# Output projection of a hybrid decoder: first readings copied by ACT, x added by DMA, low weight parts by DMA, norm scaled on demand

## The chip, the cores and the metric

The kernel runs on one core of a Trainium2 chip. The metric is the time of one execution on the device in microseconds (us); three runs of the kernel before gave 2228.88, 2226.73 and 2226.81 us, median 2226.81.

The engines by their names in the profile: PE is the matrix engine (PEld its weight loads), DVE the vector engine, ACT the scalar engine, POOL GpSimd, SP the engine that issues most DMAs. All DMAs are carried out by 16 DMA engines. DMAs that SP issues are plain copies; those that POOL issues here add their source to what stands at the destination (accumulate), on a queue of their own.

## The reference

```
for l in range(DEPTH):                      # DEPTH = 2, SEQ = D_MODEL = 1024
    h = rmsnorm(x, norm_mix_g[l])
    ... = split_cols(h @ w_in[l])           # gMLP, Mamba-2 SSD and MLA branches
    mix = concatenate([y_a, y_b, y_c])      # 1024 wide
    x = x + mix @ w_out[l]                  # the output projection
    x = x + squared_relu_mlp(rmsnorm(x, norm_mlp_g[l]), mlp_w1[l], mlp_w2[l])
return rmsnorm(x, final_norm_g)

def squared_relu_mlp(h, w1, w2):            # w1: 1024 x 4096, w2: 4096 x 1024
    return square(relu(h @ w1)) @ w2
```

All in float32.

## The kernel before

Everything is kept with features on the partitions: x is eight tiles of 128 features x 1024 tokens. Each layer has a front (norm, input projection, gMLP, SSD, attention) and then nine large products of 1024 x 1024 by 1024 x 1024, which L998 runs: the output projection `w_out` (stage 0) and, for each of four quarters of the hidden width, `w1` and `w2` (stages 1 to 8).

**A stage** (class `Stage`) is one such product by a scheme of seven block products in place of eight. Weight and activation are cut into quadrants; the seven products, numbered 1 to 7, use quadrants or running sums of quadrants, and `done(p, os)` reads the four PSUM accumulators `os` after product p and adds or subtracts them where they belong. `LATE1` and `EARLY1` are the two orders of the products; stage 0 has LATE1 (1, 5, 6, 3, 7, 2, 4), stage 1 EARLY1 (1, 2, 5, 6, 3, 7, 4). Each product has two halves kh = 0, 1. One half is a step: 4 accumulators x 2 x 3 = 24 matmuls of 128x128 by 128x512. A step is named (stage, number), number 0 to 13; (0, 10) is the first half of product 2 of the output projection. Products 1, 2, 4 and 7 load their weights into `raw` tiles (product 7 by a load and an accumulating DMA), product 5 into a tile `ssum`, which accumulating DMAs then turn into the weights of 6 and 3.

**High and low parts.** For accuracy each float32 operand is split into a high part in the type float32r, rounded (`act.copy`), and a low part, the difference (`tt(lo, src, f(hi), subtract)` on DVE). That is `split` (L114). The matmuls are high weight by high activation, high weight by low activation, low weight by high activation, in this order; so the low part of the weight (`wlo`) is read by the third matmul of a step.

**Run** (class `Run`) goes through the steps of all nine stages. Before step i it prepares weights (`prep_w`) and activations (`prep_b`) up to step i + AHEAD = i + 2. `hooks` are calls after given steps: `norm_r(0)` after (0, 10), `norm_x(0)` after (0, 11), `norm_r(1)` after (1, 0), `norm_x(1)` after (1, 1).

**x and the norm.** `mlp` loads the eight x tiles through SP (L1071) at the start of the projection. `add_to` adds each reading of stage 0 to x on DVE: 4 readings after products 1, 5, 6, 3, 2 and 4 and 8 after product 7, 32 per layer. x is complete by halves of the tokens: half 0 after product 7, half 1 after product 4. Then `after_mix` squares it (ACT) and sums the squares (DVE, POOL); `norm_r` sums over the partitions with eight small matmuls (`pss`) and takes the reciprocal root with thirteen small DVE operations (`rstd`, tiles `rv`, `ry`, `rt`); `norm_x` spreads it with eight matmuls (`rb`), copies that to SBUF (ACT), and scales all eight tiles of the half into `hB` on DVE. Stage 1 reads `hB`, half 0 from its first product, half 1 from product 5 on.

**What is scarce.** Common tiles of 128 x 1024 (`G`, 32 of them) hold x, the mixer's output, all high and low parts and sums of squares; `raw` has 4 tiles; PSUM has 8 banks, 4 with the tag "a", which the accumulators of some products, `pss` and `rb` share.

**What sets the order.** The program is written once in order of the calls; a scheduler then fixes each engine's instruction order before the run, by its own estimate of times and by free tiles and banks. On the chip each engine and each DMA queue works strictly in that fixed order.

Of the kernel before, what the change touches and what calls it, by code (L numbers as in the profile page):

```python
# [18 lines left out]
P = 128  # L19
# [42 lines left out]
SETS = ("aaaa", "bbcc")  # L62
AHEAD = 2
MIX_FROM = 36


@with_exitstack
def trunk(ctx, tc, x, w_zdk, w_uv, w_f, w_q, w_kv, w_out, w1, w2, gains, pcol, prow, w_s, cst, out):
# [182 lines left out]
    def sq_rstd(acc, tag, t0=0, t1=NT, tg="c"):  # L251
        n = t1 - t0
        pss = bank(tg, "pss")
        for t in range(t0, t1):
            for i, q in enumerate(acc):
                mm(pss[:, t * 2:t * 2 + 2], q[:, t * P:(t + 1) * P], ones[:, 0:2], i == 0, i == len(acc) - 1)
        acc.clear()
        return rstd(pss[:, 2 * t0:2 * t1:2], n, tag)
# [642 lines left out]
    class Stage:  # L901


        def __init__(self, w, src, order, done, flip=False, chain=True, tmp=None):
            self.w, self.src, self.order, self.done, self.flip = w, src, order, done, flip
            self.fresh = (1, 2, 5) if chain else (1, 2, 4, 5)
            self.tmp = tmp or (lambda name: G(F32, name))
            self.s, self.t, self.held = [None] * 2, [None] * 2, {}

# [3 lines left out]
        def prep_w(self, p, kh):  # L913
# [6 lines left out]
            hi, lo = G(F32R, "whi"), G(F32R, "wlo")  # L920
            split(hi, lo, v)
            if p in (5, 6):
# [44 lines left out]
    class Run:  # L967
        def __init__(self, stages, hooks, end):
            self.steps, self.ready, self.hooks, self.end = [], [], hooks, end
            par = 0  # L970
# [6 lines left out]

        def prep(self, n):
            while len(self.ready) < min(n, len(self.steps)):
                st, p, kh = self.steps[len(self.ready)][:3]  # L980
                self.ready.append((st.prep_w(p, kh), st.prep_b(p, kh)))

        def go(self):
            for i, (st, p, kh, v, at) in enumerate(self.steps):
                self.prep(i + 1 + AHEAD)
                (wh, wl), (bh, bl) = self.ready[i]
# [22 lines left out]
    def add_to(xt, flip=False, chain=True, hook=None):  # L1009
# [4 lines left out]
        def done(p, os):  # L1014
# [4 lines left out]
            if hook:  # L1019
                hook(p)  # L1020

        return done
# [42 lines left out]
    def mlp(L, l, xsrc):  # L1065
# [3 lines left out]
        xt = [G(F32, "x") for _ in range(KD)]  # L1069
        for m in range(KD):  # L1070
            nc.sync.dma_start(out=xt[m], in_=xsrc[m * P:(m + 1) * P, :])  # L1071
        hB, scr = [], [BIG(F32, "scr")]
        acc, rs = {}, {}
# [9 lines left out]
        def norm_r(n):  # L1083
            rs[n] = sq_rstd(acc[n], "m", n * 4, n * 4 + 4, "a")

        def norm_x(n):
            if not hB:
                scr.clear()
                hB.append(BIG(F32, "hB").rearrange("p (k t) -> p k t", k=KD))
            o = bank("a", "rb")  # L1090
            half_bcast(rs.pop(n), o)
            rb = G(F32, "rb")
            act.copy(rb[:, 0:512], o)
            for m in range(KD):
                stt(hB[0][:, m, half(n)], xt[m][:, half(n)], gcol[:, 2 * l + 1, m:m + 1], rb[:, 0:512], ALU.mult, ALU.mult)

# [82 lines left out]

        class LazyB:  # L1180
            def __getitem__(self, k):
                return hB[0][k]

        stages = [Stage(w_out[l], mix_half, LATE1, add_to(xt, True, False, after_mix), True, False, scratch)]
        for q in range(NQ):
            end = q == NQ - 1
            stages.append(Stage(w1[l, q], halves_of(LazyB()), EARLY1 if q == 0 else LATE1, relu_to(Lazy())))
            stages.append(Stage(w2[l, q], halves_of(Lazy()), LATE1,
# [3 lines left out]
        if last:  # L1192
            hooks[8, 10] = [lambda: close_r(1)]
            hooks[8, 11] = [lambda: close_x(1, 0)]

        def end():
# [157 lines left out]
```

## Time and profile before

| | before |
|---|---|
| median of three runs | 2226.81 us |
| the profiled execution | 2227.68 us |
| its span | 2225.8 us |
| busy PE / DVE / ACT / POOL | 2180.0 / 1669.2 / 1131.5 / 470.9 us |
| DMA | 222.15 MB, 39.5% of 16 engines |
| output projection and stage 1, layer 0 | about 394 to 573 us |
| the same, layer 1 | about 1490 to 1668 us |

The span is the profiler's own time from first to last instruction; the rest of the profiled execution lies around it. Busy shares are averages over stages with different limits; where PE stands is read from its waits and from the chain that ended last. The times in the trace count from the start of the span. The granted clock is a share of 2.4 GHz.

### The profile page before, as it was taken

The numbers are of one execution on the slowest core, as the hardware profiler recorded it, in microseconds if no ns is written. First come the engines' busy times: TensorE is split into PE (matmuls) and PEld (weight loads), VectorE is DVE, ScalarE is ACT, GpSimd is POOL, SyncE is SP. The second block draws the span as 40 slices with busy tenths as digits, with TensorE's granted clock in tenths as the row PEclk, the third lists the DMA queues.
The fourth block names the chain that finished last, engine by engine and source line by source line (L and its number), as shares of the span: only waits on it lengthen the run. The fifth ranks groups of instructions, "written<-read, shape, count | busy, mean of one in ns | idle before, by whom it ended". The sixth has DMA issues, their size and how long they took to land.

```text
span 2225.8 us, 28714 instructions
## 1 busy us (share of the span) xinstructions
PE 2180.0 (98%) x10844; PEld 1854.6 (83%) x10844; DVE 1669.2 (75%) x2516; ACT 1131.5 (51%) x1841; POOL 470.9 (21%) x444
## 2 busy tenths in 40 slices
PE   9999999999999999999999999999899999999996
PEld 8888989877888888888898888988788888888885
DVE  6788688788775876767847868878888767677576
ACT  6363577545445445355534626774464453543543
POOL 3152266121010001001301613751110010001011
PEclk9999999999999999999999999999999999999998
DMA  5211301354555546535412112023565465456532
GB/s 182 65 53 57 86 1 71 82 132 102 126 132 136 122 104 144 147 90 121 154 49 69 60 45 67 1 98 74 123 153 122 104 142 142 105 109 147 131 67 76
DMA packets 63625, 222.15 MB, mean 100 GB/s; under 512 B 7456, under 2 KB 7552, under 8 KB 63488
## 3 DMA queue, kind: packets, MB, share of 16 engines
q0 software_dynamic: 20736, 75.51, 19.6%
q1 hardware_dynamic: 42752, 144.83, 19.6%
q8 instruction: 85, 1.39, 0.2%
q14 instruction: 52, 0.43, 0.1%
HBM read 211.87 MB, written 8.44 MB: 99 GB/s over the span
## 4 chain that ended last, share of the span: by engine, by line
PE 94%; DVE 2%; issue 2%; ACT 1%; DMA 0%; POOL 0%; POOLq 0%; SPq 0%; ACTq 0%; DVEq 0%
PE st L998 61%; PE cqkv L119 5%; PE xbc L119 5%; PE uvps L119 4%; PE av L119 4%; PE sc L119 3%; PE zps L119 2%; PE pTp L789 2%; PE qps L119 2%; PE yps L119 1%; PE vps L119 1%; PE knps L119 1%; PE rb L119 1%; DVE mx L751 1%; DMA x<-in_x 0%
## 5 line engine op out<-in xcount | busy, mean ns | idle before, releaser
L998 PE MATMUL st<-blo,whi 128*128 128x512 f32 x2016 | 787.2, 390 | 0.0
L998 PE MATMUL st<-bhi,wlo 128*128 128x512 f32 x2016 | 786.6, 390 | 0.0
L998 PE MATMUL st<-bhi,whi 128*128 128x512 f32 x2016 | 781.4, 391 | 2.4 <-ACT bhi L115 2.4
L998 PEld LDWEIGHTS st<-bhi,whi 128*128 128x128 f32 x2016 | 380.5, 189 | 81.3 <-ACT bhi L115 2.7
L998 PEld LDWEIGHTS st<-bhi,wlo 128*128 128x128 f32 x2016 | 380.2, 189 | 79.1
L998 PEld LDWEIGHTS st<-blo,whi 128*128 128x128 f32 x2016 | 380.5, 189 | 78.3
L192 POOL DMA_DIRECT2D ssum<-in_w x96 | 84.2, 883 | 923.8 <-DVE wlo L100 380.5
L100 DVE TENSOR_TENSOR wlo<-raw,whi 128x1024 fp32r<-128x1024 f32 (+3 forms) x188 | 239.0, 1272 | 53.9 <-issue 29.8
L100 DVE TENSOR_TENSOR x<-x,st 128x512 f32<-128x512 f32 x296 | 196.0, 680 | 32.9 <-PE st L998 32.5
L115 ACT CAST bhi<-tsum 128x1024 fp32r<-128x1024 f32 x96 | 101.0, 1052 | 215.0 <-DVE tsum L100 173.9
L115 ACT CAST whi<-raw 128x1024 fp32r<-128x1024 f32 (+3 forms) x188 | 193.8, 1034 | 16.2 <-DVE blo L100 12.7
L107 POOL TENSOR_SCALAR p<-p,sm 128x1024 f32<-128x1024 f32 (+6 forms) x84 | 158.9, 1901 | 113.7 <-DVE sm L774 81.8
L115 ACT CAST whi<-ssum 128x1024 fp32r<-128x1024 f32 x108 | 113.5, 1051 | 112.2 <-PE st L998 57.1
L100 DVE TENSOR_TENSOR wlo<-ssum,whi 128x1024 fp32r<-128x1024 f32 x108 | 131.8, 1220 | 49.7 <-ACT whi L115 27.6
L100 DVE TENSOR_TENSOR blo<-tsum,bhi 128x1024 fp32r<-128x1024 f32 x96 | 117.3, 1222 | 46.4 <-ACT bhi L115 46.0
L119 PE MATMUL av<-pT,vhi 128*128 128x256 f32 x480 | 113.5, 298 | 0.8 <-DVE pT L100 0.5
L1043 ACT ACTIVATE hid<-hid 128x1024 f32<-128x1024 f32 x64 | 67.9, 1061 | 84.3 <-DVE hid L1036 84.0
L1036 DVE CUSTOM_DVE_ANT_0 hid<-st,hid 128x512 f32<-128x512 f32 x96 | 65.2, 686 | 56.8 <-PE st L998 56.5
L119 PE MATMUL sc<-B 96*128 96x384 f32 (+11 forms) x432 | 101.0, 351 | 3.1 <-ACT p L764 1.8
L100 POOL TENSOR_TENSOR sq<-sq 128x512 f32<-128x512 f32 (+1 forms) x37 | 60.7, 1647 | 191.9 <-ACT sq L1055 179.9
L100 DVE TENSOR_TENSOR blo<-hB,bhi 128x1024 fp32r<-128x1024 f32 x48 | 58.7, 1223 | 48.5 <-ACT bhi L115 48.5
L764 ACT ACTIVATE p<-sc,mx 128x512 f32<-128x512 f32 (+3 forms) x144 | 83.2, 583 | 21.0 <-DVE mx L100 14.2
(244 smaller groups left out, 3647.2 us busy)
## 6 DMA issues: line engine op xcount, KB each, us to landing
raw<-in_w SPq DMA_DIRECT2D x128, 512.0 KB, 3.7
ssum<-in_w POOLq DMA_DIRECT2D x96, 512.0 KB, 5.7
ssum<-in_w SPq DMA_DIRECT2D x32, 512.0 KB, 4.5
raw<-in_w POOLq DMA_DIRECT2D x32, 512.0 KB, 9.3
raw<-in_w_f SPq DMA_DIRECT2D x20, 512.0 KB, 3.5
x<-in_x SPq DMA_DIRECT2D x16, 512.0 KB, 6.9
raw<-in_w_out SPq DMA_DIRECT2D x16, 512.0 KB, 3.7
dec<-adr SPq DMA_DIRECT2D x16, 384.0 KB, 3.5
```

What stands on the lines that cost most here:

```text
L100: (eng or dve).tensor_tensor(out=o, in0=a, in1=b, op=op)
L107: (eng or dve).tensor_scalar(out=o, in0=a, scalar1=s1, scalar2=None, op0=op0)
L115: act.copy(hi, src)
L119: pe.matmul(o, lhsT=l, rhs=r, start=start, stop=stop)
L192: pool.dma_start(out=o, in_=src, accum_op=ALU.add)
L751: dve.reduce_max(mx[:, n:n + 1], on, axis=AX.X, negate=True)
L764: act.activation(pw[:, n * wh:(n + 1) * wh], os[n][:, :wh], AF.Exp, bias=mx[:, 0:1], accum_out=sm[:, n:n + 1])
L789: pe.transpose(pt[:, c0:c0 + P], pp[j][:, kt * P:(kt + 1) * P], ident)
L998: pe.matmul(os[j], lhsT=w[:, cw], rhs=b[:, cb], start=first and n == 0, stop=last and n == 2, skip_group_check=True)
L1036: dve._custom_dve(TENSOR_ADD_SAT, out=d, in0=os[j], in1=d, s0=0.0 if full[0] else BIGGEST, s1=-BIGGEST if full[0] else 0.0)
L1043: act.activation(d, d, AF.Square)
```

## The change

Six edits, all in the output projection (stage 0) and the first MLP product (stage 1) of each layer.

1. `make` takes the place of `add_to` in stage 0. The first reading of each quadrant (after products 1, 5, 6 and 7) is copied from PSUM into the x tile by ACT, with the sign; then an accumulating DMA on POOL's queue adds the old x from memory. The second readings (after 3, 7, 2 and 4) are added by DVE as before. The eight loads of x through SP are gone.
2. In stages 0 and 1 (`by_dma`) the low parts of the weights of products 1, 2, 4 and 7 are no longer a DVE subtraction: ACT writes the negated high part into `wlo` and an accumulating DMA adds the weight, from memory, or for product 7 from the raw tile.
3. `norm_x` no longer scales the eight tiles at once; `normed` scales two tiles when a step of stage 1 first asks for them.
4. `norm_r` and `norm_x` use one PSUM bank for `pss` and `rb` where they had one each.
5. `Run.prep` prepares weights and activations with separate leads; before the steps in `SHORT` the activations are prepared one step ahead instead of two.
6. One tile `rb` is kept for both halves.

```diff
--- before.py
+++ after.py
@@ -61,6 +61,7 @@
 SAME = {LATE1: (0, 1, 0, 1, 0, 1, 0), EARLY1: (0, 1, 1, 0, 1, 0, 0)}
 SETS = ("aaaa", "bbcc")
 AHEAD = 2
+SHORT = ((0, 9), (0, 10), (0, 11), (0, 13), (1, 0), (1, 1))
 MIX_FROM = 36
 
 
@@ -250,7 +251,7 @@
 
     def sq_rstd(acc, tag, t0=0, t1=NT, tg="c"):
         n = t1 - t0
-        pss = bank(tg, "pss")
+        pss = bank(tg, "pss") if isinstance(tg, str) else tg
         for t in range(t0, t1):
             for i, q in enumerate(acc):
                 mm(pss[:, t * 2:t * 2 + 2], q[:, t * P:(t + 1) * P], ones[:, 0:2], i == 0, i == len(acc) - 1)
@@ -905,6 +906,8 @@
             self.w, self.src, self.order, self.done, self.flip = w, src, order, done, flip
             self.fresh = (1, 2, 5) if chain else (1, 2, 4, 5)
             self.tmp = tmp or (lambda name: G(F32, name))
+            self.parts = None
+            self.by_dma = False
             self.s, self.t, self.held = [None] * 2, [None] * 2, {}
 
         def b(self, b, n, kh):
@@ -918,7 +921,12 @@
             else:
                 v = self.s[kh]
             hi, lo = G(F32R, "whi"), G(F32R, "wlo")
-            split(hi, lo, v)
+            if self.by_dma and p in (1, 2, 4, 7):
+                act.copy(hi, v)
+                act.activation(lo, f(hi), AF.Copy, scale=-1.0)
+                gather(lo, v if p == 7 else self.w[LOADS[p][0] + (kh,)])
+            else:
+                split(hi, lo, v)
             if p in (5, 6):
                 gather(v, self.w[0, p - 5, kh])
             elif p == 3:
@@ -966,7 +974,7 @@
 
     class Run:
         def __init__(self, stages, hooks, end):
-            self.steps, self.ready, self.hooks, self.end = [], [], hooks, end
+            self.steps, self.w, self.ready, self.hooks, self.end = [], [], [], hooks, end
             par = 0
             for n, st in enumerate(stages):
                 sets = [par ^ v for v in SAME[st.order]]
@@ -975,14 +983,18 @@
                     for kh in range(2):
                         self.steps.append((st, p, kh, v, (n, 2 * i + kh)))
 
-        def prep(self, n):
-            while len(self.ready) < min(n, len(self.steps)):
+        def prep(self, n, m=None):
+            while len(self.w) < min(n, len(self.steps)):
+                st, p, kh = self.steps[len(self.w)][:3]
+                self.w.append(st.prep_w(p, kh))
+            while len(self.ready) < min(m or n, len(self.steps)):
                 st, p, kh = self.steps[len(self.ready)][:3]
-                self.ready.append((st.prep_w(p, kh), st.prep_b(p, kh)))
+                self.ready.append((self.w[len(self.ready)], st.prep_b(p, kh)))
+                self.w[len(self.ready) - 1] = None
 
         def go(self):
             for i, (st, p, kh, v, at) in enumerate(self.steps):
-                self.prep(i + 1 + AHEAD)
+                self.prep(i + 1 + AHEAD, i + 1 + (1 if at in SHORT else AHEAD))
                 (wh, wl), (bh, bl) = self.ready[i]
                 self.ready[i] = None
                 fresh = p in st.fresh
@@ -1021,6 +1033,27 @@
 
         return done
 
+    def make(xt, xsrc, flip, hook):
+        first = {1: (0, 0), 5: (1, 1), 6: (0, 1), 7: (1, 0)}
+        then = {3: (0, 1), 7: (1, 1), 2: (0, 0), 4: (1, 0)}
+
+        def done(p, os):
+            if p in then:
+                a, n = then[p]
+                for j in range(4):
+                    v = xt[a * 4 + j][:, half(n ^ flip)]
+                    tt(v, v, os[j], ALU.subtract if a else ALU.add)
+            if p in first:
+                a, n = first[p]
+                for j in range(4):
+                    m = a * 4 + j
+                    v = xt[m][:, half(n ^ flip)]
+                    act.activation(v, os[j], AF.Copy, scale=-1.0 if a else 1.0)
+                    gather(v, xsrc[m * P:(m + 1) * P, half(n ^ flip)])
+            hook(p)
+
+        return done
+
     def relu_to(hid):
         def done(p, os):
             def v(a, n, j):
@@ -1067,9 +1100,7 @@
         mix = L.mixA + L.mixC
         L.mixA = L.mixC = None
         xt = [G(F32, "x") for _ in range(KD)]
-        for m in range(KD):
-            nc.sync.dma_start(out=xt[m], in_=xsrc[m * P:(m + 1) * P, :])
-        hB, scr = [], [BIG(F32, "scr")]
+        hB, rb, have, scr = [], [], set(), [BIG(F32, "scr")]
         acc, rs = {}, {}
         slot = [0]
 
@@ -1081,18 +1112,28 @@
             return [mix[b * 4 + kh * 2 + kk][:, half(n)] for kk in range(2)]
 
         def norm_r(n):
-            rs[n] = sq_rstd(acc[n], "m", n * 4, n * 4 + 4, "a")
+            o = bank("a", "rb")
+            rs[n] = sq_rstd(acc[n], "m", n * 4, n * 4 + 4, o), o
 
         def norm_x(n):
             if not hB:
                 scr.clear()
                 hB.append(BIG(F32, "hB").rearrange("p (k t) -> p k t", k=KD))
-            o = bank("a", "rb")
-            half_bcast(rs.pop(n), o)
-            rb = G(F32, "rb")
-            act.copy(rb[:, 0:512], o)
-            for m in range(KD):
-                stt(hB[0][:, m, half(n)], xt[m][:, half(n)], gcol[:, 2 * l + 1, m:m + 1], rb[:, 0:512], ALU.mult, ALU.mult)
+                rb.append(G(F32, "rb"))
+            r, o = rs.pop(n)
+            half_bcast(r, o)
+            act.copy(rb[0][:, half(n)], o)
+
+        def normed(b, n, kh):
+            m0 = b * 4 + kh * 2
+            for m in range(m0, m0 + 2):
+                if (m, n) not in have:
+                    have.add((m, n))
+                    stt(hB[0][:, m, half(n)], xt[m][:, half(n)], gcol[:, 2 * l + 1, m:m + 1], rb[0][:, half(n)],
+                        ALU.mult, ALU.mult)
+            if len(have) == 2 * KD:
+                rb.clear()
+            return (hB[0][:, m0:m0 + 2, half(n)],)
 
         def after_mix(p):
             if p == 3:
@@ -1177,14 +1218,10 @@
                     hid.append(BIG(F32, "hid").rearrange("p (k t) -> p k t", k=KD))
                 return hid[0][k]
 
-        class LazyB:
-            def __getitem__(self, k):
-                return hB[0][k]
-
-        stages = [Stage(w_out[l], mix_half, LATE1, add_to(xt, True, False, after_mix), True, False, scratch)]
+        stages = [Stage(w_out[l], mix_half, LATE1, make(xt, xsrc, True, after_mix), True, False, scratch)]
         for q in range(NQ):
             end = q == NQ - 1
-            stages.append(Stage(w1[l, q], halves_of(LazyB()), EARLY1 if q == 0 else LATE1, relu_to(Lazy())))
+            stages.append(Stage(w1[l, q], normed, EARLY1 if q == 0 else LATE1, relu_to(Lazy())))
             stages.append(Stage(w2[l, q], halves_of(Lazy()), LATE1,
                                 add_to(xt, False, not end, (finish if last else to_next) if end else None), chain=not end))
         hooks = {(0, 10): [lambda: norm_r(0)], (0, 11): [lambda: norm_x(0)],
@@ -1192,6 +1229,9 @@
         if last:
             hooks[8, 10] = [lambda: close_r(1)]
             hooks[8, 11] = [lambda: close_x(1, 0)]
+
+        for st in stages[:2]:
+            st.by_dma = True
 
         def end():
             if not last:
```

## Rows read from the trace of the kernel before

**Rows 1.** The page: the chain that ended last, by engine.

```profile
PE 94%; DVE 2%; issue 2%; ACT 1%; DMA 0%; POOL 0%; POOLq 0%; SPq 0%; ACTq 0%; DVEq 0%
```

**Rows 2.** PE's waits, layer 0 and 1 (waiter, releaser: total us, times, longest).

```profile
PE rb L119 <- DVE ry L103: 7.0, 2, 4.6
...
PE rb L119 <- DVE ry L103: 7.0, 2, 4.5
```

**Rows 3.** DVE in order of time (start us, us, instruction, idle before it).

```profile
447.17 0.69 DVE L100 TENSOR_TENSOR x<-x,st 128x512 f32<-128x512 f32 x1 [0.67 <-PE st L998]
448.53 0.69 DVE L100 TENSOR_TENSOR x<-x,st 128x512 f32<-128x512 f32 x1 [0.67 <-PE st L998]
...
455.89 2.47 DVE L100 TENSOR_TENSOR x<-x,st 128x512 f32<-128x512 f32 x4
...
469.86 0.69 DVE L100 TENSOR_TENSOR x<-x,st 128x512 f32<-128x512 f32 x1 [0.66 <-PE st L998]
...
471.45 1.18 DVE L100 TENSOR_TENSOR rt<-ry 128x4 f32<-128x4 f32 x1
...
478.55 5.39 DVE L103 SCALAR_TENSOR_TENSOR hB<-x,gcol,rb 128x512 f32<-128x512 f32 x8 [2.85 <-ACT rb L1093]
```

**Rows 4.** The chain in order of time (start us, us, what).

```profile
475.76 2.08 PE rb L119 x8
477.84 23.71 PE st L998 x96
...
504.77 1.27 PE rb L119 x8
506.04 599.93 PE st L998 x2640
...
1135.32 0.89 PE rb L119 x8
```

**Rows 5.** Stretch, us, busy PE, PEld, DVE, ACT, POOL, granted clock, DMA share, GB/s.

```profile
452.00:506.00 54.00, 47.02 (x210) 39.10 (x209) 44.23 (x74) 23.69 (x32) 7.27 (x7) 0.93 0.54 137
```

**Rows 6.** Groups of instructions (busy us, mean ns of one, idle before).

```profile
L100 DVE TENSOR_TENSOR x<-x,st 128x512 f32<-128x512 f32 x296 | 196.0, 680 | 32.9 <-PE st L998 32.5
...
L100 DVE TENSOR_TENSOR wlo<-ssum,whi 128x1024 fp32r<-128x1024 f32 x108 | 131.8, 1220 | 49.7 <-ACT whi L115 27.6
...
L1039 ACT COPY hid<-st 128x512 f32<-128x512 f32 x96 | 56.0, 583 | 31.5 <-PE st L998 31.0
```

**Rows 7.** SP's queue and POOL in order of time.

```profile
376.69 7.43 SPq L1071 DMA_DIRECT2D x<-in_x  x8
...
390.14 5.97 POOL L107 TENSOR_SCALAR p<-p,sm 128x896 f32<-128x896 f32 x2 [1.58 <-DVE sm L774]
...
475.23 1.78 POOL L192 DMA_DIRECT2D ssum<-in_w  x2
```

**Rows 8.** DMA view, 390 to 452, 547 to 571: packets, MB, share; landing.

```profile
ssum<-in_w_out POOLq DMA_DIRECT2D x4, 512.0 KB, 5.8
...
q0 software_dynamic: 720, 2.62, 56.4%
q1 hardware_dynamic: 766, 2.74, 31.5%
...
ssum<-in_w POOLq DMA_DIRECT2D x3, 512.0 KB, 9.4
```

**Rows 9.** ACT and PE in order of time.

```profile
391.07 1.06 ACT L115 CAST whi<-raw 128x1024 fp32r<-128x1024 f32 x1
...
394.29 0.50 PE L998 MATMUL st<-bhi,whi 128*128 128x512 f32 x1 [1.19 <-ACT bhi L115]
...
449.79 1.03 ACT L115 CAST whi<-raw 128x1024 fp32r<-128x1024 f32 x1
```

**Rows 10.** DMA view, 452 to 506: packets, MB, share of 16 engines.

```profile
q1 hardware_dynamic: 1440, 5.24, 30.6%
q0 software_dynamic: 576, 2.10, 22.7%
```

## Prediction, made before the changed kernel was built or run

> **What bounds the kernel now.** I read the chain of work first: PE makes up 94% of the chain [rows 1]. In such a kernel time is won only where PE stands or runs slowly, so the next view is PE's waits, stretch by stretch. The change touches the output projection and the first MLP stage of each layer, and there PE waits for one thing: the broadcast of the norm (tile `rb`) waits for the reciprocal root `ry` on DVE, twice in each layer, 7.0 us together, the longer one 4.6 us [rows 2]. The reader is to see there that both layers show the same pair.
>
> The cost of these waits is more than their idle time. One accumulator j takes 6 matmuls, and at full clock DVE gets the next one every 1.36 us (447.17 and 448.53) [rows 3], so a matmul takes 0.2267 us and a step (24 matmuls, one half of one of the seven products) 5.44 us. Behind the first wait the eight broadcast matmuls take 2.08 us, where a pair without a wait takes 0.89, and the next 96 matmuls take 23.71 us instead of 96 x 0.2267 = 21.76 [rows 4]. The granted clock shows why: a mean of 0.93 from 452 to 506 us [rows 5], so part of that stretch ran at 1.2 and not 2.4 GHz. First wait: 4.6 + 1.19 + 1.95 = 7.7 us. Second: 2.4 + (1.27 - 0.89) + (599.93 - 2640 x 0.2267) = 2.4 + 0.4 + 1.4 = 4.2 us [rows 2, 4]. That is 11.9 us in layer 0; layer 1 has the same two waits [rows 2] and I give it the same, 23.8 us in all, 1.07% of the time. Nothing else in the stages concerned can give time back, since PE is otherwise fed.
>
> **The change part by part.** *The norm.* The last product of each half of x is added by DVE, then come squares, the sums `pss` on PE, thirteen small DVE operations, and `rb`. In the first wait x additions stood between the small operations (469.86), some of which took 1.18 us (471.45), and `rb` could start only at 475.76 [rows 3, 4]; in the second the same chain took the bare 2.4 us of the wait [rows 2]. After the change product 7 has four DVE additions instead of eight, 4 x 0.60 us less (the four at 455.89 took 2.47 us together [rows 3]), and the two low parts that DVE made just there are gone too (1.22 us each [rows 6]). The squares are so ready about 2.4 us sooner, which brings `pss` from the middle of step (0,11) towards its start, with nearly a whole step (5.44 us) for a chain of 2.4 to 4 us. The bank that `pss` and `rb` now share is one allocation less between product 7 and product 4, so the matmuls of the next step can be placed ahead of a late `rb`. For the second norm the eight scalings in one piece of 5.39 us (478.55) [rows 3] become two before each step that needs them; these are the same operations, spread out, and DVE has room: 44.23 us busy of 54 [rows 5], and it loses more than it gains. I cost the scaling at zero and expect both waits to go: minus 11.9 us per layer. With a lead of one step in place of two for six operand preparations (SHORT), copy, subtraction and two scalings (1.05 + 1.22 + 2 x 0.7 = 3.7 us) must fit in 5.44 us; queued behind them on DVE are only the additions of that step. Zero, and up to 1 us per layer if they queue badly.
>
> *x by DMA.* 16 DVE additions (680 ns) per layer become 16 ACT copies (583 ns [rows 6]) and 16 accumulating DMAs of 256 KB on POOL's queue; eight loads of 512 KB leave SP's queue at 376.69 [rows 7]. ACT is busy 23.69 us of 54 [rows 5] and gets 4 copies and 8 further passes there, 4 x 0.58 + 8 x 1.05 = 10.7 us: covered. Each x piece is added to again only two steps later at the earliest (product 6, then 3), 10.9 us for an accumulating DMA that alone lands 5.8 us after its issue [rows 8]: covered.
>
> *Low parts by DMA.* Per layer 16 DVE subtractions become 16 ACT passes (about 1.05 us [rows 9]) and 16 accumulating DMAs of 512 KB. The matmul that reads the low part is the third of its step, so the wait that is added stands in PE's own queue. The tightest place by time alone is step (0,10): high part at 449.79 [rows 9], need at 448.5 + 2 x 5.44 + 0.45 = 459.8. Copy, negation and landing take 1.05 + 1.05 + 5.8 = 7.9 us: on time by 2 us, if the DMA finds the engines free. POOL gets 32 further issues of about 0.9 us per layer (its two at 475.23 took 1.78 [rows 7]), in order behind its square sums.
>
> The engines are not free, and this is my main term. An accumulating DMA of 512 KB (a gather, as the code calls it) occupies the 16 DMA engines for longer than a load: from 452 to 506 four gathers made 22.7% of 54 us, 3.06 us each, and ten loads 30.6%, 1.65 each [rows 10]. Where the engines are crowded (547 to 571, share 56.4 + 31.5%), five gathers took 2.71 us each, and 766 packets (144 to a load) 1.42 us per load, and landing stretched from 5.8 to 9.4 us [rows 8]; the work of both queues adds up there. I use the crowded values. From 452 to step (1,3) the new kernel has 4 old gathers, the low parts of eight steps, (0,10) to (1,3), and four x pieces of half size: 14 x 2.71 = 37.9 us, with at least 8 of the ten loads, 11.4 us: 49.3 us. Of the lone landing of 5.8 us some 2.7 are no transfer; I put 1.4 ahead of it and 1 behind. So it starts at about 451.9 + 1.4 = 453.3 and has landed near 503.6. Without waits step (1,3) would need its low part at 506.04 - 10.5 + 5.44 + 0.5 = 501.5 (10.5 is 11.9 less the 1.4 lost behind 506): late by 2.1 us at least. By order it can be worse: ahead of the low part of step (1,0) stand four low parts, the x pieces, and the two gathers that POOL issued at 475.23 [rows 7]: 9 x 2.71 + 7 loads x 1.42 = 34.3 us, landed at 488.6, needed at 477.84 + 1.95 + 2 x 5.44 - 7.7 + 0.45 = 483.4, 5.2 us late; four gathers on, step (1,2) adds 1.3. If those two gathers go behind it, it is on time. So PE stands still 2.1 to 6.5 us per layer; middle 4.3. Such a stand costs clock too: 1.8 us behind the wait of 2.4 us, 3.1 behind the one of 4.6 (above), none if it comes in small pieces. I take 1.8. Given back: 6.1 us of 11.9 per layer, so 5.8 us net, 11.6 for both. The bounds: 2.1 + 0 leaves 19.6 us net, 6.5 + 3.1 leaves 4.6.
>
> *The sum.* The profiled execution took 2227.68 us around a span of 2225.8, 0.9 above the median; the differences are taken off the median: 2226.8 - 11.6 = **2215**, between 2207 and 2222.
>
> **The rivals.** *All of it is won.* Both waits go and each low part lands after the lone 5.8 us [rows 8], since PE needs it only 9.9 us or more after its high part starts. 2226.8 - 23.8 = 2203, 2200.6 with the 1.19 us as well that PE stands at the first step of each layer [rows 9]. Against it: the landing of 9.4 us where queues were full. The Trainium skill (DMA: Bandwidth & Descriptors, Anatomy of one DMA) fits a gpsimd DMA by 2.0 us + bytes / 436e3, an estimate of 3.2 us for 512 KB. By that this rival would hold and the time would be 2203; the trace shows 5.8 us, and 2.7 us of engine time in a crowd, so I follow the rows.
>
> *Nothing moves.* The order on PE is fixed before the run. If `pss` and `rb` keep their places, the waits stay and hide the late low parts, since 52 us of DMA work fits in the old 54. 2222 to 2231.
>
> *Slower: the first step's low part.* Step (0,0) begins at 394.29 [rows 9]. Its high part was cast at 391.07; negated by 393.1, its DMA would stand behind POOL's scaling until 396.1 [rows 7] and land at 401.9, needed at 394.8: 7.1 us, with 3.1 of clock 10.2 us per layer. With 6.1 given back later, that is 16.3 - 11.9 = 4.4 us per layer lost: 2236. It decides if the cast stays at 391. Against it: eight tiles of the common pool no longer go to x at 376.69 [rows 7], so cast and negation can be done some 10 us sooner.
>
> **How the numbers follow.** Part won 0.38 (2207 to 2222), all won 0.27 (2200 to 2207), nothing moves 0.12 (2222 to 2231), slower 0.23 (2231 to 2241). A measurement of this kernel tells 0.2%, 4.5 us, from no change. Faster is 0.38 + 0.27 = 0.65, the same 0.12, slower 0.23. From 2200 to 2235 leaves out some 0.14 above and 0.03 below. The likeliest alone is 2215.
>
> **What would show it.** Right: PE's waits no longer name `rb <- ry`, but `st` waiting for the DMA of `wlo` near steps (0,12), (1,0) and (1,2); the DMA share from 452 on is above 0.85; gathers land in 7 to 12 us. All won: no PE wait over 1 us, clock 1.00 throughout. Wrong: `rb` still waits, or the first wait of `st` is at the start of the projection. If the DMA share stays near 0.6, my engine times for a gather are too long.

## The result: slower by 1.3%, and the profile after

The changed kernel took 2257.98 us (median of four runs, 2251.64 to 2258.78) against 2226.77 us: ratio 1.013, 95% interval 1.0117 to 1.0142. The profiled execution took 2257.24 us around a span of 2255.4 (before 2227.68 and 2225.8). The forecast of 2215 was wrong in sign, and its range, up to 2235, did not hold the time.

First the page: the chain that ended last, by engine; beside [rows 1], PE fell from 94% to 86%, issue rose from 2% to 5% and DMA from 0% to 3%.

```profile
PE 86%; issue 5%; DMA 3%; DVE 2%; ACT 2%; POOL 1%; POOLq 0%; SPq 0%; ACTq 0%; DVEq 0%
```

PE's waits after, in layer 0 from 390 to 580 us, those of the stages' matmuls `st` (waiter, releaser: total us, times, longest):

```profile
PE st L1010 <- DMA wlo<-in_w_out: 7.6, 2, 4.8
PE st L1010 <- ACT bhi L116: 3.9, 3, 2.1
PE st L1010 <- DMA wlo<-in_w: 3.8, 1, 3.8
PE st L1010 <- DVE blo L101: 1.5, 1, 1.5
```

The two waits of `rb` for `ry`, 7.0 us [rows 2], are gone, and the matmuls `st` wait 16.8 us, where they waited 1.2 us before, at the first step [rows 9]. The larger part, 11.4 us, is for low weight parts that come by DMA; 5.4 us is for activations: 0.7 at the first step, the rest at steps (0,13), whose operand is queued behind the norm's work, and (1,4), which the norm feeds. Layer 1 has much the same list (5.9, 3.9, 3.2 and 1.7 us), and 0.6 us more for a low part made from a raw tile.

The stretches, to set beside [rows 5] (stretch, us, busy PE, PEld, DVE, ACT, POOL, granted clock, DMA share, GB/s):

```profile
390.00:452.00 62.00, 59.68 (x308) 50.28 (x307) 33.21 (x45) 38.22 (x58) 23.58 (x23) 1.00 0.73 136
452.00:506.00 54.00, 43.85 (x184) 34.87 (x183) 28.42 (x52) 32.24 (x43) 19.49 (x20) 0.91 0.91 204
506.00:540.00 34.00, 28.15 (x107) 21.84 (x106) 20.68 (x33) 12.98 (x16) 2.61 (x3) 0.85 0.46 102
```

and of the kernel before the two stretches that [rows 5] leaves out:

```profile
390.00:452.00 62.00, 60.34 (x316) 51.39 (x317) 46.96 (x63) 32.39 (x50) 13.37 (x9) 1.00 0.32 71
...
506.00:540.00 34.00, 34.00 (x145) 28.00 (x144) 30.78 (x32) 19.66 (x24) 3.47 (x4) 0.95 0.40 65
```

From 452 to 506 us DVE is relieved as intended (28.42 us against 44.23), but the DMA engines are busy for 0.91 of the stretch against 0.54, and PE works 43.85 us against 47.02. The granted clock is 0.91 and then 0.85, so part of these stretches ran at 1.2 and not 2.4 GHz; before it was 0.93 and 0.95.

How the first late low part came about is seen in order of time. ACT, DVE, POOL and PE after the change (start us, us, instruction, idle before it):

```profile
444.95 0.61 ACT L1051 ACTIVATE x<-st 128x512 f32<-128x512 f32 x1
...
447.75 0.69 DVE L101 TENSOR_TENSOR x<-x,st 128x512 f32<-128x512 f32 x1 [1.43 <-DMA x<-in_x]
...
449.28 0.88 POOL L193 DMA_DIRECT2D x<-in_x  x1 [0.42 <-PE st L1010]
...
451.78 0.69 DVE L101 TENSOR_TENSOR x<-x,st 128x512 f32<-128x512 f32 x1 [2.02 <-DMA x<-in_x]
455.56 0.69 DVE L101 TENSOR_TENSOR x<-x,st 128x512 f32<-128x512 f32 x1 [3.09 <-DMA x<-in_x]
...
456.28 0.63 ACT L1088 ACTIVATE sq<-x 128x512 f32<-128x512 f32 x1 [3.15 <-DVE x L101]
456.82 1.03 ACT L925 CAST whi<-raw 128x1024 fp32r<-128x1024 f32 x1
457.88 1.06 ACT L926 ACTIVATE wlo<-whi 128x1024 fp32r<-128x1024 f32 x1
...
459.35 0.88 POOL L193 DMA_DIRECT2D wlo<-in_w_out  x1 [0.99 <-ACT wlo L926]
...
465.79 0.80 PE L1010 MATMUL st<-bhi,wlo 128*128 128x512 f32 x1 [4.83 <-DMA wlo<-in_w_out]
```

Read it upwards. Step (0,10) waits 4.83 us for its low part. POOL issued that DMA at 459.35, because ACT made the high part only at 456.82; in the kernel before that was 449.79 [rows 9]. ACT came late because four squares of x stand ahead in its order. They wait for DVE's additions of product 3, and these wait for the x pieces of product 6, which are now DMAs. ACT copied the last of these pieces at 444.95, POOL issued its DMA at 449.28, and DVE could add to it at 455.56.

### The profile page after: what moved, and what is told of

Read it like the earlier page. It is cut to its first block, busy times and chain, and to the rows that moved or that the text cites. A ratio compares the mean times of both kernels' runs of the same rounds, so it can differ in the third digit from the quotient of the medians.

```text
span 2255.4 us, 28761 instructions
## 1 busy us (share of the span) xinstructions
PE 2193.4 (97%) x10844; PEld 1858.3 (82%) x10844; DVE 1610.2 (71%) x2452; ACT 1178.1 (52%) x1905; POOL 527.4 (23%) x508
## 4 chain that ended last, share of the span: by engine, by line
PE 86%; issue 5%; DMA 3%; DVE 2%; ACT 2%; POOL 1%; POOLq 0%; SPq 0%; ACTq 0%; DVEq 0%
PE st L1010 54%; PE cqkv L120 5%; PE xbc L120 5%; PE uvps L120 4%; PE av L120 3%; PE sc L120 3%; PE zps L120 2%; PE pTp L790 2%; PE qps L120 2%; PE yps L120 1%; DMA wlo<-in_w 1%; DMA wlo<-in_w_out 1%; PE vps L120 1%; PE knps L120 1%; DMA x<-in_x 1%
## 5 line engine op out<-in xcount | busy, mean ns | idle before, releaser
L101 DVE TENSOR_TENSOR wlo<-raw,whi 128x1024 fp32r<-128x1024 f32 (+3 forms) x156 | 201.5, 1293 | 50.6 <-issue 29.8
L101 DVE TENSOR_TENSOR x<-x,st 128x512 f32<-128x512 f32 x264 | 175.7, 682 | 42.5 <-PE st L1010 27.4
L116 ACT CAST whi<-raw 128x1024 fp32r<-128x1024 f32 (+3 forms) x156 | 160.3, 1032 | 16.9 <-DVE blo L101 12.0
```

What stands on the lines that cost most here:

```text
L101: (eng or dve).tensor_tensor(out=o, in0=a, in1=b, op=op)
L116: act.copy(hi, src)
```

## The experiments

Each ratio is to runs of the kernel before on the same chip, median 2227.1 to 2227.6 us.

| run | us | ratio, 95% interval |
|---|---|---|
| e1_x_and_norm | 2236.12 | 1.0033 (1.0022 to 1.0044) |
| e2_lo_and_norm | 2242.98 | 1.0065 (1.0050 to 1.0080) |
| e3_norm_only | 2233.33 | 1.0024 (1.0015 to 1.0034) |
| e4_small_dmas | 2218.44 | 0.9955 (0.9940 to 0.9970) |
| e5_no_short | 2233.75 | 1.0030 (1.0019 to 1.0042) |
| e6_on_demand | 2227.69 | 1.0003 (0.9993 to 1.0012) |
| e7_one_bank | 2238.31 | 1.0047 (1.0032 to 1.0062) |
| e8_larger_ring | 2253.71 | 1.0113 (1.0096 to 1.0130) |
| e9_half_bytes | 2228.58 | 1.0004 (0.9994 to 1.0013) |
| e10_short_two_banks | 2215.84 | 0.9950 (0.9935 to 0.9965) |
| e11_short_four | 2223.82 | 0.9983 (0.9974 to 0.9992) |
| e12_two_low | 2214.94 | 0.9944 (0.9930 to 0.9959) |
| e13_small_sums | 2220.28 | 0.9965 (0.9952 to 0.9978) |
| e14_four_small | 2215.76 | 0.9948 (0.9931 to 0.9964) |

### Which part costs: four runs

**e1**, the change without edit 2:

```diff
-        for st in stages[:2]:
-            st.by_dma = True
```

> The changed kernel with the low parts of the weights made by DVE again; x by DMA and the norm edits stay. Theory A (the accumulating DMAs ask for more of the 16 DMA engines than there is between 440 and 515 us, and the low parts are most of it): ten gathers of 2.7 us fall out of that stretch, no wait of st for wlo is left, the late squares of the first norm (they waited for x to land) come in time, and the time is 2203 to 2212 us, faster than before. Rival B (the x pieces alone do the harm, because the squares on ACT stand in order behind them): x still lands late, ACT's high part of step (0,10) still starts after 455 us, and the time stays above 2235 us.

**e2**, the change without edit 1:

```diff
+        for m in range(KD):
+            nc.sync.dma_start(out=xt[m], in_=xsrc[m * P:(m + 1) * P, :])
-        stages = [Stage(w_out[l], mix_half, LATE1, make(xt, xsrc, True, after_mix), True, False, scratch)]
+        stages = [Stage(w_out[l], mix_half, LATE1, add_to(xt, True, False, after_mix), True, False, scratch)]
```

> The changed kernel with x loaded through SP at the start and added by DVE as before; low parts by DMA and the norm edits stay. Theory A: the low parts keep the engines crowded, but 24 us of x gathers per layer are gone: 2215 to 2235 us, with PE waits for wlo left. Rival B: without x gathers nothing blocks ACT, the low parts land in time, 2203 to 2210 us.

**e3**, both diffs together, so edits 3 to 6 alone:

> The changed kernel with neither x nor low parts by DMA: only the scaling on demand, the shared bank and the late preparation (SHORT). If these edits alone remove the two waits for rb (11.9 us per layer with the clock): 2203 to 2210 us. Rival C: DVE's part of the old tail (eight additions and two low parts) was needed for the waits to go, and SHORT makes steps (0,13) and (1,4) wait for their activations by 2 to 5 us per layer: 2218 to 2232 us.

**e4**, the change with tiny DMAs:

```diff
-                gather(lo, v if p == 7 else self.w[LOADS[p][0] + (kh,)])
+                gather(lo[:, 0:32], (v if p == 7 else self.w[LOADS[p][0] + (kh,)])[:, 0:32])
```

and the like for the x pieces.

> The changed kernel in which each new accumulating DMA, low parts and x, moves 32 columns in place of 1024 or 512, so that the low parts and x are wrong in the rest; every instruction, wait and the order on POOL stay. Theory A (bytes crowd the DMA engines): DMA share falls to about 0.5 in 440 to 515 us, PE's waits for wlo are gone, 2203 to 2212 us. Rival D (not the bytes but the chain of ACT passes, POOL's order and the fixed landing time): the waits stay within 30%, and the time stays above 2240 us.

The norm edits alone cost about 6 us instead of bringing 24. On top of them x by DMA costs 2.8 us (the intervals of e1 and e3 overlap, so this one is hardly told from nothing), the low parts 9.7, and both 24.7: more than the sum of 12.5, so the two hinder each other. In e1 PE waits for no low weight part; x still lands late (DVE's additions wait 5.9 us for it), but ACT makes the high part of step (0,10) at 453.59, where it was 456.82. So e1 has the time that rival B named without the cast after 455 us that B asks for, e2 is slower than both its theories said, and e3 is 1.3 us slower than rival C's range. The ranges of e1 and e2 had taken the norm edits for a gain.

With the same instructions and 32 columns in each DMA (e4) the kernel is faster than before; the bytes of these DMAs cost 2257.98 - 2218.44 = 39.5 us. PE's order is not quite the same there: it differs in 285 of 10,844 places, mostly before 440 us, where the last matmuls of the attention are woven in; POOL's and SP's orders are the same. Even so the gain over the kernel before is 9.0 us and not 23.8, and PE still waits 6.0 us in layer 0 for activations.

What the norm edits alone did is seen in PE's order of e3, layer 0 (lines as above; the first `rb` line of each norm is the sums, whose bank now bears that name):

```profile
464.83 0.95 PE L120 MATMUL rb<-ones,sq 128*128 128x2 f32 x8
475.31 1.05 PE L120 MATMUL rb<-cs,ry 128*128 128x128 f32 x8
...
484.78 0.79 PE L1010 MATMUL st<-blo,whi 128*128 128x512 f32 x1 [3.67 <-DVE blo L101]
...
508.81 1.05 PE L120 MATMUL rb<-cs,ry 128*128 128x128 f32 x8
518.83 2.07 PE L1010 MATMUL st<-bhi,whi 128*128 128x512 f32 x4 [3.72 <-ACT bhi L116]
```

and in DVE's:

```profile
477.07 5.39 DVE L104 SCALAR_TENSOR_TENSOR hB<-x,gcol,rb 128x512 f32<-128x512 f32 x8 [3.59 <-ACT rb L1127]
482.38 1.22 DVE L101 TENSOR_TENSOR wlo<-raw,whi 128x1024 fp32r<-128x1024 f32 x1
483.51 1.22 DVE L101 TENSOR_TENSOR blo<-scr,bhi 128x1024 fp32r<-128x1024 f32 x1
```

The broadcast no longer waits. It stands so far behind its sums (42 and 49 matmuls in PE's order, where it was 9 and 0) that the operands behind it are late: 3.67 us at step (0,13), 3.72 at (1,4). And "on demand" hardly happens: for the first norm the scheduler puts all eight scalings in one block of 5.39 us, as before [rows 3], and for the second seven of eight.

### Which norm edit: three runs

**e5** is e3 with `SHORT = ()`.

> The norm edits alone (x loaded by SP and added by DVE as before, low weight parts by DVE as before), with SHORT empty, so that every activation is again prepared two steps ahead. The norm edits with SHORT took 2233.3 us: DVE made the eight scalings in one block of 5.39 us ahead of the low activation part of step (0,13), and PE waited 3.67 us for that; the like 3.72 us at step (1,4). If SHORT put the scalings ahead of that low part (theory S), the wait at (0,13) goes, 3.67 us and some clock per layer, and the time is 2220 to 2227. If the scaling block is late whatever the lead is (rival: the shared bank or the tile rb set the order), it stays at 2231 to 2235.

**e6** is e5 with a bank each for `pss` and `rb`, so the scaling by two tiles alone.

> As the run above, and pss and rb have a bank each as in the kernel before: what is left of the change is the scaling two tiles at a time. If the shared bank lets the matmuls of the broadcast slip behind a step (theory B), the second broadcast goes back to directly behind its chain, the wait of 3.7 us at step (1,4) goes, and PE waits for the broadcast again as before, about 2.4 and up to 4.6 us per layer: 2222 to 2230. If the bank decides nothing, the time is that of the run above within 3 us, with no wait of the broadcast.

**e7**, the kernel before with one bank:

```diff
-            rs[n] = sq_rstd(acc[n], "m", n * 4, n * 4 + 4, "a")
+            o = bank("a", "rb")
+            rs[n] = sq_rstd(acc[n], "m", n * 4, n * 4 + 4, o), o
```

> The kernel before with one edit: pss and rb share a PSUM bank. If the shared bank is what takes the two waits of the broadcast away (theory B), these waits (7.0 us per layer) are not in the trace, and the time is 2215 to 2225, unless the eight scalings in one piece are then what PE waits for (a wait for the activation's high or low part near steps (0,13), (1,0) or (1,4), time 2225 to 2235). If the bank decides nothing, the two waits stay and the time is 2225 to 2229.

Theory S falls: without SHORT the waits are still there (4.2 and 5.7 us), the time is the same. Theory B holds. Scaling by two tiles with two banks is the kernel before (2227.69; the waits of `rb` are 7.0 us again, the block of eight takes 5.39 us), and the bank alone costs 11 us, 3 us more than the slowest case that I had given it. PE in e7, layer 0:

```profile
469.51 0.95 PE L119 MATMUL rb<-ones,sq 128*128 128x2 f32 x8
...
489.61 0.50 PE L998 MATMUL st<-blo,whi 128*128 128x512 f32 x1 [4.23 <-DVE blo L100]
...
509.52 1.05 PE L119 MATMUL rb<-cs,ry 128*128 128x128 f32 x8
521.03 2.07 PE L998 MATMUL st<-bhi,whi 128*128 128x512 f32 x4 [6.80 <-ACT bhi L115]
```

Two waits of 7.0 us became two of 11.0.

### Bytes or issue: two runs

**e8**, more room for the descriptors of POOL's DMAs, every engine's order unchanged:

```diff
-    nc = _bacc.Bacc("TRN2", target_bir_lowering=False, num_devices=1, dynamic_dma_scratch_size=1024)
+    nc = _bacc.Bacc("TRN2", target_bir_lowering=False, num_devices=1, dynamic_dma_scratch_size=1792)
```

> The changed kernel with one number altered: the memory set aside for the descriptors of POOL's DMAs is 1792 instead of 1024. Every engine's order of instructions is that of the changed kernel. POOL issues some of its DMAs late there although their operands are ready (4.0 to 4.5 us after the negation of a low part at 473.71 and 477.83). If POOL waits for room for descriptors (theory R: about three accumulating DMAs of 512 KB under way at most), the issues come sooner, the waits for low parts shrink by up to those 4 us each, and the time falls by 5 to 15 us, to 2243 to 2253. If only the bytes of the DMA engines bound it (theory A), the landing gets longer by as much as the issue is sooner, and the time stays within 3 us of 2258.

**e9** is e4 with half of the columns in place of 32.

> The changed kernel with half of the bytes in each new accumulating DMA: 256 of 512 columns of x, 512 of 1024 columns of a low part; what the rest would add is left out. The number of DMAs, POOL's order and all other engines stay. With 32 columns the time was 2218.4 us, with all 2258.0. If the time goes with the bytes as such (each DMA's own landing, theory L), half of them give about half of the 39.5 us: 2236 to 2241. If the 16 DMA engines are full and only what exceeds their time costs (theory A; 0.91 busy from 452 to 506 us with all bytes, 0.64 with 32 columns, so some 0.78 with half), most of the loss goes at half: 2220 to 2230.

In e8 POOL does issue sooner: its last x piece of product 6 goes out at 442.60 instead of 449.28, that is 0.35 us after ACT's copy ended and not 3.72, and the two low parts that the text above names go out 0.35 us after their negation ended, where they had stood 4.9 and 6.0 us (the 4.0 to 4.5 above are misread). The wait at (0,10) falls from 4.83 to 1.51 us, and the time by 4.3 us (the intervals of the two ratios, 1.0096 to 1.0130 and 1.0117 to 1.0142, overlap). But x pieces now land after 9.3 us (median) instead of 6.2, and the next low part is late by 4.63 us. So theory R is right as a mechanism and small in size; most of the loss stays.

In e9 (PE's order differs as in e4) half of the bytes cost 10.1 us over e4, the other half 29.4: this is theory A's curve, not theory L's line. My figure for the share was wrong (0.78 expected, 0.89 measured from 452 to 506). The DMA views from 440 to 520 us, of the changed kernel, e9 and e4 in turn (packets, MB, share of 16 engines):

```profile
q0 software_dynamic: 3445, 10.20, 69.7%
q1 hardware_dynamic: 1728, 6.29, 23.1%
...
q0 software_dynamic: 3380, 6.35, 46.9%
q1 hardware_dynamic: 1728, 6.29, 25.1%
...
q0 software_dynamic: 3379, 3.22, 28.5%
q1 hardware_dynamic: 1728, 6.29, 24.2%
```

With half of the bytes the engines have 58 of 80 us of work and PE waits 4.3 us for low parts of `in_w` in the whole run (7.0 with all bytes) and 0.69 us in layer 0 for those of `in_w_out` (7.6); with all they have 74, which leaves little room in which a late DMA could be caught up.

### What the norm edits can bring: three runs

**e10** is e6 with the SHORT of the change: two banks, nothing by DMA.

> The norm edits with a bank each for pss and rb: SHORT and the scaling by two tiles stay, x and low parts as before the change. In PE's order the sums then stand 24 matmuls ahead of the broadcast in both norms (9 and 0 in the kernel before; 42 and 49 with SHORT and the shared bank). If the shared bank is what makes the consumers of the norm late (theory B), the wait of 3.7 us at step (1,4) goes, the second broadcast waits under 1 us, the first about 2.4 us (its chain of small operations ended 8 us after its sums in the run of the norm edits alone, and 24 matmuls are 5.4), and what is left is the late low part of step (0,13), put off by SHORT, about 3.3 us: 2219 to 2227. If SHORT alone makes them late, 2230 to 2235.

**e11** is e10 with a shorter list:

```diff
+SHORT = ((0, 9), (0, 10), (0, 13), (1, 0))
```

> As the run above with SHORT cut to (0,9), (0,10), (0,13) and (1,0): the low activation part of step (0,13) is prepared ahead of the scalings again, and the sums stay 24 and 20 matmuls ahead of the broadcast. If the sums' place in PE's order and the order of DVE are all there is to the two waits (theory B with S), the second wait goes (4.2 us per layer by the prediction's count), the first shrinks from 4.6 to 2 to 3 us, and no new wait of an activation appears: 2209 to 2217. If shortening a lead always brings a wait of its own, 2224 to 2232.

**e12** is e11 with two low parts per layer by DMA:

```diff
-            if self.by_dma and p in (1, 2, 4, 7):
+            if p in self.by_dma:
...
+        stages[0].by_dma = (4,)
```

> As the run above, and two of the low weight parts of each layer, those of product 4 of the output projection, come by DMA as in the change (2 accumulating DMAs of 512 KB per layer in place of 32, of which 16 were half as large). DVE then has the chain of small operations of the first norm ahead of the x additions. If the bytes were what cost the change its gain, two DMAs find the engines free (0.54 busy in that stretch before), and both waits are gone: 2203 to 2210, faster than the run above by 3 us or more. If each such DMA brings a wait of its own however few there are, PE waits for the low part at steps (0,12) and (0,13), and the time is that of the run above or more, 2211 to 2222.

PE in e10, layer 0:

```profile
466.26 0.95 PE L120 MATMUL pss<-ones,sq 128*128 128x2 f32 x8
474.93 1.16 PE L120 MATMUL rb<-cs,ry 128*128 128x128 f32 x8 [2.12 <-DVE ry L104]
485.10 0.50 PE L1010 MATMUL st<-blo,whi 128*128 128x512 f32 x1 [1.71 <-DVE blo L101]
494.34 0.95 PE L120 MATMUL pss<-ones,sq 128*128 128x2 f32 x8
501.68 1.16 PE L120 MATMUL rb<-cs,ry 128*128 128x128 f32 x8 [0.79 <-DVE ry L104]
```

The edit that I had priced at "Zero, and up to 1 us per layer" brings the gain: against e6, SHORT is worth 11.9 us, better than I expected of e10. With it the scheduler puts the sums 24 matmuls, one step, ahead of each broadcast. The squares are ready hardly sooner (DVE's last sum of the first norm ends at 464.6 in e10 and at 465.1 in e6); it is the place of `pss` in PE's order that moved, and why the scheduler moves it is not shown. e12 is as fast as e10 (no difference can be told between them): both beat the kernel before by 0.5%, and the changed kernel by some 42 us. e12 fell short of the 2203 to 2210 that I expected: its first wait is gone, but the second stands at 1.66 us, because DVE puts three subtractions (2.35 and 1.22 us) between the small operations there; 0.51 us is a wait for a low part.

e11 was a miss, 2223.8 us. Its second wait is 0.68 us as expected, its first 5.01 us:

```profile
476.12 2.07 PE L120 MATMUL rb<-cs,ry 128*128 128x128 f32 x8 [5.01 <-DVE ry L104]
```

### What the first wait is made of: two runs

The small operations are twelve in the traces (thirteen in the text ahead), and some of them took four to seven times as long as the others. Beside the 1.18 us at 471.45 in [rows 3] POOL shows this in the kernel before:

```profile
469.89 1.29 POOL L100 TENSOR_TENSOR sq<-sq 128x512 f32<-128x512 f32 x1 [18.55 <-ACT sq L1055]
471.35 1.26 POOL L100 TENSOR_TENSOR sq<-sq 128x512 f32<-128x512 f32 x1 [0.17 <-ACT sq L1055]
474.03 1.26 POOL L100 TENSOR_TENSOR sq<-sq 128x512 f32<-128x512 f32 x1 [1.42 <-ACT sq L1055]
```

Each slow operation ends within 0.05 us of one of these: 470.46 + 0.75, 471.45 + 1.18, 474.12 + 1.19. **e13** is the kernel before with only that changed:

```diff
+            c = slice(n * 512, n * 512 + 8) if small else half(n)
-            tt(acc[0][:, half(n)], acc[0][:, half(n)], sq[:, half(n)], ALU.add, eng)
+            tt(acc[0][:, c], acc[0][:, c], sq[:, c], ALU.add, eng)
...
-                    sq_half(acc[1], xt[m], m, 1, pool)
+                    sq_half(acc[1], xt[m], m, 1, pool, True)
```

> The kernel before with one edit: POOL's three sums of squares after product 2 of the output projection (the sums for the second half of the tokens) take 8 of 512 columns; the rest of these sums is left out. The order on every engine is that of the kernel before. If POOL's sums hold up DVE's small operations (theory P), these take 0.16 us each where they took 0.75, 1.18 and 1.19, together 2.6 us less, the first wait of the broadcast falls from 4.6 to about 2.0 us, and with the clock that the longer wait cost the time falls by 2.6 to 4.5 us per layer: 2218 to 2222. If they are slow on their own account, the wait stays at 4.6 and the time at 2225 to 2229.

**e14** is e11 with the same edit.

> The run with SHORT cut to four and two banks (2223.8 us), with the same edit of POOL's three sums. Four small operations took 0.85 to 1.11 us there, 3.5 us more than 0.16 each. By theory P the first wait falls from 5.0 to about 1.5 us and the time to 2214 to 2219. Otherwise it stays at 2222 to 2226.

POOL, DVE and PE in e13:

```profile
470.67 0.20 POOL L100 TENSOR_TENSOR sq<-sq 128x8 f32<-128x8 f32 x1 [1.25 <-ACT sq L1055]
...
471.56 0.16 DVE L100 TENSOR_TENSOR rt<-ry 128x4 f32<-128x4 f32 x1
...
472.15 0.16 DVE L100 TENSOR_TENSOR rt<-ry 128x4 f32<-128x4 f32 x1
...
472.76 1.16 PE L119 MATMUL rb<-cs,ry 128*128 128x128 f32 x8 [2.23 <-DVE ry L103]
```

Theory P holds. The order of every engine is the same, all small operations take 0.15 to 0.17 us, the first wait is 2.23 us instead of 4.55, and the time falls by 7.3 us, 3.6 per layer. In e14 the first wait falls to 2.44 us (1.5 were expected) and the time by 8.1 us. Half of the first wait, and e11's miss, is DVE held up by POOL's sums. e12 escapes them without that edit: with two subtractions fewer, DVE is through with the small operations before POOL begins. The block of eight scalings stands beside POOL's sums there and takes 7.13 us in place of 5.39.

The Trainium skill (SBUF — State Buffer, SBUF: two separate sides) says that DVE and GpSimd share a pair of SBUF ports, and that a GpSimd operation, or a DVE operation in a two-port mode or with two inputs in SBUF, whichever starts first, holds it to its end while the other waits. The traces agree, also in what is not held up: the x addition at 469.86 [rows 3], one of whose inputs is in PSUM, took its usual 0.69 us beside POOL's sum at 469.89, and that sum took 1.29, where the two behind it took 1.26. The operation at 470.46 has one input in SBUF; whether it ran in a two-port mode no run here shows.

## Why the prediction was wrong, step by step

**The marks came as told, the sizes did not.** Of what was to show the forecast right, nearly all was seen: `rb` no longer waits for `ry`, `st` waits for `wlo` (at steps (0,10), (0,12) and (1,2); told were (0,12), (1,0) and (1,2)), the DMA share is 0.91, low parts of `in_w_out` and `in_w` land after 7.3 and 9.7 us (medians). The time moved the other way all the same.

**The step that failed first: "x by DMA: covered".** It set the lone landing of 5.8 us against 10.9 us, two steps of PE. The landing was right, about 6 us for the pieces of product 6. The 10.9 us were not there: ACT's copies stood behind its casts, the last at 444.95, 3.6 us ahead of where the last addition of product 3 stood before (448.53 [rows 3]), and POOL issued that piece only at 449.28, for want of room for descriptors as e8 showed. So the additions of product 3 waited 1.43, 2.02 and 3.09 us. Through ACT's fixed order this moved the high part of (0,10) by 7.0 us, which the sum for the low parts had kept at 449.79.

**The main term, mis-sized.** The time of the DMA engines was about right: from 440 to 520 us q0 moved 10.20 MB, 19.5 gathers, in 0.697 x 80 = 55.8 us, 2.87 us each (taken: 2.71), and 12 loads took 18.5 us, 1.54 each (taken: 1.42). Wrong was the start: I let the engines begin at 453.3 with nothing in hand, while their share was already 0.73 from 390 to 452 (0.32 before), and I carried no lateness from one step to the next. Told were 2.1 to 6.5 us of waiting and 1.8 of clock per layer; PE waited 11.4 us in layer 0 and 9.7 in layer 1 for low parts, and e4 puts the bytes at 39.5 / 2 = 19.8 us per layer, where the sum had 6.1.

**The norm, wrong in sign.** "I cost the scaling at zero and expect both waits to go: minus 11.9 us per layer." The waits of `rb` went and came back behind it. The sentence that failed is the one on the shared bank: matmuls did go ahead of a late broadcast, as it said, and I did not ask who waits behind the work that the broadcast releases. Edits 3 to 6 brought plus 3 us per layer (e3). The premise that sooner squares bring sooner sums was wrong too. In the kernel before, the squares of the first half were summed at 463.4, and `pss` stood 4.7 us further on in PE's order, with no wait ahead of it:

```profile
461.88 1.48 DVE L100 TENSOR_TENSOR sq<-sq 128x512 f32<-128x512 f32 x2
...
468.06 0.95 PE L119 MATMUL pss<-ones,sq 128*128 128x2 f32 x8
```

**The price of the two waits** was of the right size, if somewhat high: in e12, 7.0 us of waiting became 2.2 and the time fell by 12.4 us, 6.2 per layer, where 11.9 x 4.8 / 7.0 would be 8.2. What they consist of I had wrong in part: x additions between the small operations were named, and the 1.18 us at 471.45 were left without a cause, which was POOL's hold (e13).

**The rivals.** "All of it is won" fell with the landing, 7.3 us for low parts of `in_w_out`, and with it the estimate of 3.2 us worked out from the Trainium skill (DMA: Bandwidth & Descriptors, Anatomy of one DMA). "Nothing moves" fell with its condition: sums and broadcast stand 37 and 42 matmuls apart after the change, 9 and 0 before. "Slower" had the sign, at the wrong place. Its condition came true, and my argument against it did not: the cast stayed at 390.41 (391.07 before), and the low part's DMA went out behind POOL's scaling, as told. But PE does not wait for it, since the scheduler had put matmuls of the attention ahead of the one that reads it, at 401.29, where it stood at 395.67 before:

```profile
394.78 0.88 POOL L193 DMA_DIRECT2D wlo<-in_w_out  x1
...
401.29 0.40 PE L1010 MATMUL st<-bhi,wlo 128*128 128x512 f32 x1
```

At the first step PE waits 0.68 us, for an activation, less than before (1.19 [rows 9]).

## What to carry to other kernels

When a transfer is called covered, count its margin from the instruction that starts it, take its issue time and the engine's backlog into account as well as its landing, and follow each waiting instruction along its engine's fixed order; near full DMA engines lateness adds up, and the second half of the bytes cost three times the first. A wait that vanishes from one instruction is won only if what that instruction feeds comes earlier too: move the producer up (SHORT, two banks), not the consumer back. And where a small operation takes several times its usual time, look at what the neighbouring engine does in that microsecond.

## What was not expected of the hardware

- A 1.26 us sum on POOL held DVE operations on 128x4 elements for up to 1.19 us; three of them were worth 3.6 us per layer.
- With more room for descriptors (e8) accumulating DMAs that had gone out 3.7 to 6.0 us after their operands were made went out 0.35 us after, with POOL's order unchanged, so that room had set their issue; the landing of x pieces grew from 6.2 to 9.3 us.
- Waits of 2.12, 1.71 and 0.79 us within 27 us left the granted clock at 1.00 from 452 to 506 us in e10, all of it at 2.4 GHz; with one wait of 4.55 us and one of 2.43 it was 0.93 before.
